# A decoder trunk on one core: the second MLP product's queues in the order of emission, its raw weight halves kept by use, and two mixer weights read into rows of another tile

## The chip, the cores and the metric

The kernel is one program for one core of one Trainium2 chip. The metric is the device time of one execution in microseconds (us); lower is better. Before the change it is 2401.24 us, the median of three runs (2396.24 to 2403.47).

The engines are called by the names of the profile: PE multiplies matrices (PEld is its weight load), DVE and ACT do elementwise work, POOL does a few small things, and SP issues nearly all transfers (DMAs) between the core's memory and DRAM. Each engine runs its own instructions in a fixed order and waits at the first whose inputs or buffers aren't ready. Matmuls write into PSUM, which has eight banks of 128x512 numbers; DVE and ACT have to read a bank out ("evict" it) before PE may start another sum in it.

## The reference

Two layers on a residual stream of 1024 positions by 1024 channels. What matters here is the MLP, which both layers have, and the weights of the second layer's attention:

```python
def _sqrelu_mlp(x, w_up, w_down):                       # 1024 -> 4096 -> 1024
    return jnp.square(jax.nn.relu(x @ w_up)) @ w_down
...
for i in range(DEPTH):
    m = gmlp(...) if i % 2 == 0 else diff_attention(...)   # attention: qkv = a @ w_qkv
    h = h + _rmsnorm(m, g_mix_post[i])
    f = _sqrelu_mlp(_rmsnorm(h, g_ffn_pre[i]), f_w_up[i], f_w_down[i])
    h = h + _rmsnorm(f, g_ffn_post[i])
    gate = jax.nn.sigmoid(_rmsnorm(h, g_ple_pre[i]) @ ple_w_gate[i] + ple_b_gate[i])
    e = gate * (p[i] @ ple_w_proj[i])
    h = h + _rmsnorm(e, g_ple_post[i])
```

## The kernel before

**Arithmetic.** Everything is fp32. Each operand is cut into a high part (ACT copies it to the matmul's type) and a low part (DVE subtracts the high part from the whole), and each product is three matmuls, high by high, high by low and low by high (lines 352 to 354 in `mm3`, line 364 in `proj_steps`). Cutting one operand is thus one ACT and one DVE instruction: `cut` in `ffn` (line 523 on ACT, line 524 on DVE), `split` for the other stages (lines 113 to 120).

**The MLP** is `ffn`, called once per layer. Both of its products are done with seven half-size products in place of eight, so sums and differences of blocks have to be formed. The first product (`product`, `block`) forms blocks of the hidden activations, squares them and stores seven kinds of them to DRAM (`hid`). The banks of the first product are read out by `plus` (line 601), on DVE.

**The second product** is the loop at line 810. It has 56 steps in four groups: groups 0, 1 and 2 have 16 steps each (steps 0 to 47), group 3 has 8. In each step PE does 24 matmuls of 128x128 by 128x512: four output rows `p`, two banks each, three matmuls per bank. All eight banks are in use: `PM[p]` and `other[p]` hold one group's sums through its 16 steps. After a group's last step `evict(g, p)` reads the two banks of each row out into halves of the rows of `MA` (lines 785 to 796): one ACT and one DVE instruction per row in group 0, two DVE ones in group 1 (lines 789 and 790), three in group 2. The next group's first matmul into a bank has to wait for that.

**Feeding the steps.** For step `n`, `load_down(n)` issues the transfers and `split_down(n)` does the arithmetic. The call `after(t)`, at the end of step `t`, first calls `split_down` for the step that is `lead_s` ahead (two in group 0, three in groups 1 and 2) and then `load_down` for the one that is `lead_l` ahead (seven through step 50). The places that the cut operands go to are seven rooms, used in turn, so the loads of step `n` into its room have to wait for PE to be done with step `n - 7`. In `load_down`, group by group:

- groups 0 and 1: a whole row block of the weight (512 KB, line 727) and one half of another (256 KB, line 728) into a set of raw buffers, and a slice of `hid` (512 KB, line 729) into the room;
- group 2: two halves (256 KB each, line 724) and a half `t4` that group 1 has stored to DRAM (256 KB, line 725) into raw buffers, and the slice of `hid`.

The raw buffers of a group are a ring of sets in `sets` (five in groups 0 and 1, in the order of the steps; four in group 2). A set is one whole 128x1024 buffer and one half of a row of `MA`.

`split_down` forms two differences on DVE (lines 746 and 747 in group 1, 753 and 754 in group 2), issues a store of one of them to `t4` from SP in the middle of its own work (lines 748 and 755), and cuts three pieces: the `hid` slice (128x1024) and two weight halves (128x512).

**What sets the order.** The code emits instructions in the order of its loops, but only PE keeps that order (the whole trunk stands in `tc.manual_schedule(engines={PE})`, line 1319). The order on SP, ACT, DVE and POOL is made when the program is built, by a planner that takes instructions as it expects them to be ready, the earlier emitted first among those that are. On the chip this order is then fixed. Inside a block of `manual_schedule` the instructions of the engines that it names keep their order of emission among themselves; instructions emitted outside the block may still be placed between them.

**Around it.** In group 3 and after it, `half` and `whole` scale and sum the rows, add them to the residual and prepare the next stage, whose transposes (line 296) PE does when `settle` asks for them or when `tick` has counted far enough.

**Mixer weights.** The other stages read their weights through `ws` (`WStream`): `load` reads a 512 KB block (line 88) into the next of a ring of raw buffers and splits it into one of six slots, and `take` hands four of them out. At the start of `mixer1` (line 1158) the first two blocks of `w_qkv` are already in their slots; the other two of the first four are loaded when `qkv_qk` first calls `take`, through the ring `[raw, hin[0], hin[1]]` set at line 1165. `hin` also holds the residual rows of the stage before (`residual`, lines 336 to 342). The rows of `MA` hold that stage's outputs until PE has transposed them, row by row.

Of the kernel before, what the change touches and what calls it, by code (L numbers as in the profile page):

```python
# [21 lines left out]
NT = T // P  # L22
# [3 lines left out]
NQ = DFF // FB  # L26
# [17 lines left out]
def f32(ap):  # L44
    return ap.bitcast(F32)
# [86 lines left out]
def _trunk(ctx, tc, nc, a, out):  # L132
# [14 lines left out]
    MA = sp.tile([P, NT, D], F32, name="ma")  # L147
    WT = [sp.tile([P, 2, D], F32, name=f"w{i}") for i in range(4)]
    hin = [sp.tile([P, D], F32, name=f"hin{i}") for i in range(2)]
# [116 lines left out]
    def settle(key=None):  # L266

        while put_off and (key is None or any(k == key for k, _, _ in put_off)):
            put_off.popleft()[2]()
# [245 lines left out]
    def ffn(i, hsrc, hdst, next_weights):  # L515
# [6 lines left out]
        def cut(h, l, v):  # L522
            act(h, v, AF.Copy)  # L523
            vec(out=l, in0=v, in1=f32(h), op=sub)  # L524
# [124 lines left out]
        def stream():  # L649
            for q in range(NQ):  # L650
                if q < 3:
                    settle((4, 6, 7)[q])
                yield from load_up(q)

        LEAD = 6
        loads = stream()
        early = [(q, n) for qs in ((0, 1), (2,), (3,), (4,)) for n in (1, 2) for q in qs]
        stage = [x.rearrange("p (r k f) -> p r k f", r=2, f=P) for x in (raw, bbc, raw, bbc, bbc)]
# [37 lines left out]
        def cols(x, k):  # L696
            return x[:, k * 512:k * 512 + 512]
# [1 line left out]
        sets = [  # L699
            Ring([(MA[:, 1], cols(MA[:, 2], 0)), (MA[:, 3], cols(MA[:, 2], 1)), (raw, cols(MA[:, 4], 0)),  # L700
                  (MA[:, 5], cols(MA[:, 4], 1)), (MA[:, 6], cols(bbc, 0))]),
            Ring([(x, cols(MA[:, t], 1)) for t, x in zip((0, 7, 2, 3, 4), hin + [xn[0], raw, bbc])]),
            Ring([(x, cols(MA[:, t], 1)) for t, x in zip((6, 5, 4, 7), [hin[1], raw, bbc, hin[0]])]),
        ]


        sumR = Ring([cols(xn[1], k) for k in range(2)])
        steps = [(g, c) for g in range(4) for c in range(NQ if g < 3 else NQ // 2)]
        loaded, cuts, ssq = {}, {}, {}

        def load_down(n):
            g, c = steps[n]
            room = last[c] if g == 3 else rooms[n % 7]
            hi, lo = [f32r(x.rearrange("p k t -> p (k t)")) for x in room]
            wh, hh, wl, hl = hi[:, 0:1024], hi[:, 1024:], lo[:, 0:1024], lo[:, 1024:]
            x = sets[g].next() if g < 3 else None
            if g == 3:
                for k in range(2):
                    nc.sync.dma_start(f32(cols(hl, k)), hid[2 * c + k][:, 3072:])
                nc.sync.dma_start(f32(wl), t4[c])  # L720
            else:
                if g == 2:
                    for k in range(2):
                        nc.sync.dma_start(cols(x[0], k), down[c, k, 1])
                    nc.sync.dma_start(x[1], cols(t4[c // 2], c % 2))
                else:
                    nc.sync.dma_start(x[0], down_rows[c, 0])
                    nc.sync.dma_start(x[1], down[c, 1, 1 - g])
                nc.sync.dma_start(f32(hl), hid[c][:, g * 1024:g * 1024 + 1024])
            loaded[n] = wh, wl, hh, hl, x  # L730

        def split_down(n):
            g, c = steps[n]
            wh, wl, hh, hl, x = loaded.pop(n)
            if g < 3:
                a1, a2 = cols(x[0], 0), cols(x[0], 1)
            if g == 0:

                t = sumR.next()
                vec(out=t, in0=a2, in1=a1, op=sub)  # L740
                vec(out=a2, in0=x[1], in1=t, op=sub)
                w = x[0],
            elif g == 1:

                t = sumR.next()
                vec(out=t, in0=a2, in1=a1, op=sub)
                vec(out=a1, in0=x[1], in1=a1, op=sub)
                nc.sync.dma_start(cols(t4[c // 2], c % 2), a1)
                w = x[1], t
            elif g == 2:  # L750

                t = sumR.next()
                vec(out=t, in0=a2, in1=a1, op=sub)
                vec(out=x[1], in0=x[1], in1=t, op=sub)
                nc.sync.dma_start(cols(t4[c // 2], c % 2), x[1])
                w = t, a2
            else:
                w = f32(wl),
            cut(hh, hl, f32(hl))
            k = D // len(w)  # L760
            for j, v in enumerate(w):
                cut(wh[:, j * k:j * k + k], wl[:, j * k:j * k + k], v)
            cuts[n] = wh, wl, hh, hl

        def after(t):

            for n in range(len(steps)):
                if n - t == lead_s[n]:
                    split_down(n)
            for n in range(len(steps)):  # L770
                if n - t == lead_l[n]:
                    load_down(n)

        for k, n in enumerate(rest_of):
            next(loads, None)
# [28 lines left out]
        def whole(tt, us):  # L804
# [2 lines left out]
            rstd_of(s[:, 0:1], D, RMS_EPS)  # L807
            residual(tt, MA[:, tt, :], s[:, 0:1], hsrc, hdst, us)

        for m, (g, c) in enumerate(steps):  # L810
            wh, wl, hh, hl = cuts.pop(m)
            n_c = NQ if g < 3 else NQ // 2

# [344 lines left out]
    def mixer1(gi, hsrc, hdst):  # L1158
# [3 lines left out]
        nc.gpsimd.dma_start(sgc, a["subln"])  # L1162
        nc.vector.tensor_scalar(out=sgc, in0=sgc, scalar1=1.0 - LAMBDA_INIT, scalar2=None, op0=ALU.mult)
        pbR.i = 2 * (pmR.i % 3)
        ws.raws = Ring([raw] + hin)
        for cb in range(2):
            qkv_qk(cb, qD, HD ** -0.5, cosT, sinT)
# [267 lines left out]
```

## Time and profile before

| what | value |
| --- | --- |
| median of three runs | 2401.24 us |
| the profiled execution: time, span in the profile | 2402.34 us, 2400.6 us |
| DVE busy over the span | 1609.3 us (67%) |
| ACT busy over the span | 1165.4 us (49%) |
| second product of layer 0, steps 0 to 55 | about 606 to 938 us |
| second product of layer 1, steps 0 to 55 | about 1951 to 2280 us |
| end of the gate stage, start of `mixer1` | about 1055 us |

All times inside the profile are us from the start of the span. In a timeline row the first number is the start, the second the duration, then come engine, line, operation, tiles (written <- read) and shape; the bracket at the end is the time that the engine was idle just before, and what ended it. In a row of waits stand the engine, tile and line that waited, what ended the wait, the us in total, the number of times and the longest. A row of windows gives, for a stretch, the busy time and the number of instructions of each engine, the granted PE clock (1.00 is full), the share of the 16 DMA engines and GB/s. Matmuls overlap, so a busy duration of 0.39 us goes with a distance of about 0.23 us between starts.

### The profile page before, as it was taken

Reading aid. Unit: us, or ns where it says so; the run is one execution under the profiler, and the core shown is the slowest. Engines: PE = TensorE matmul, PEld = TensorE weight load, DVE = VectorE, ACT = ScalarE, POOL = GpSimd, SP = SyncE. Lnnn points to the kernel's source line nnn. Section 1 sums busy time; section 2 is a strip of 40 time slices with the busy share of each in tenths; the row PEclk is TensorE's granted clock in tenths of the full one; section 3 lists DMA queues with packets and bytes.
Section 4 is the critical chain, followed back from the end, with each engine's and each line's share of the span. In section 5 each row is a group of like instructions: output and inputs, shape, how many; then the busy total and the mean of one; then the engine's idle time right before and its main releaser. Section 6 shows DMA issues by size and latency. Waiting matters only on the chain. (4 is left out here: it accounts for less than half of the span.)

```text
span 2400.6 us, 30544 instructions
## 1 busy us (share of the span) xinstructions
PE 2327.9 (97%) x10748; PEld 1924.2 (80%) x10748; DVE 1609.3 (67%) x2492; ACT 1165.4 (49%) x2003; POOL 228.0 (9%) x303
## 2 busy tenths in 40 slices
PE   9999999999999899999999989999999999989998
PEld 7888888888788687878887878777888888868787
DVE  4733697777866765563335888868877797675654
ACT  6232575555433355462224666657555554334551
POOL 1100100000000022010001342321000000000310
PEclk9999999999999999999999999999999999999999
DMA  9111545446977765244445765554544588777423
GB/s 330 57 35 54 165 142 202 145 156 223 355 249 236 250 233 183 74 169 142 147 154 179 218 181 143 158 184 137 189 159 164 173 335 279 243 256 245 176 106 123
DMA packets 200425, 441.03 MB, mean 184 GB/s; under 512 B 21040, under 2 KB 55856, under 8 KB 200144
## 3 DMA queue, kind: packets, MB, share of 16 engines
q1 hardware_dynamic: 199840, 437.89, 54.4%
q8 instruction: 85, 1.39, 0.2%
q0 software_dynamic: 432, 1.19, 0.2%
q14 instruction: 68, 0.56, 0.1%
HBM read 310.02 MB, written 133.17 MB: 185 GB/s over the span
## 5 line engine op out<-in xcount | busy, mean ns | idle before, releaser
L364 PE MATMUL pm_a<-w,xh 128*128 128x512 f32 x704 | 223.9, 396 | 1.3 <-ACT w L119 0.9
L364 PEld LDWEIGHTS pm_a<-w,xh 128*128 128x128 f32 x704 | 131.6, 189 | 29.8 <-ACT w L119 2.6
L523 ACT ACTIVATE xh<-xl 128x1024 fp32r<-128x1024 f32 x72 | 75.4, 1055 | 148.9 <-DMA xl<-hid 137.5
L364 PE MATMUL pb<-w,xh 128*128 128x512 f32 x416 | 134.9, 400 | 5.5 <-DVE gbc L972 2.9
L524 DVE TENSOR_TENSOR xl<-xl,xh 128x1024 fp32r<-128x1024 f32 x72 | 87.4, 1221 | 78.6 <-ACT xh L523 75.6
L364 PE MATMUL pm_a<-w,xl 128*128 128x512 f32 x352 | 138.7, 394 | 0.0
L523 ACT ACTIVATE w<-ma 128x512 fp32r<-128x512 f32 x130 | 82.2, 634 | 115.6 <-PE pm_a L353 39.5
L524 DVE TENSOR_TENSOR s<-s 128x1024 fp32r<-128x1024 f32 x56 | 68.0, 1222 | 58.9 <-ACT s L523 58.9
L523 ACT ACTIVATE s<-s 128x1024 fp32r<-128x1024 f32 x56 | 58.5, 1054 | 97.6 <-DMA s<-hid 80.6
L847 POOL DMA_DIRECT2D bbc<-in_ple_b_gate_dram x2 | 1.3, 628 | 1077.1 <-DVE s L524 1077.1
L353 PE MATMUL pm_a<-xl,w 128*128 128x512 f32 x260 | 101.4, 390 | 0.2 <-DVE xl L283 0.2
L352 PE MATMUL pm_a<-xh,w 128*128 128x512 f32 x260 | 101.6, 391 | 0.0
L354 PE MATMUL pm_a<-xh,w 128*128 128x512 f32 x260 | 101.2, 389 | 0.0
L364 PEld LDWEIGHTS pb<-w,xh 128*128 128x128 f32 x416 | 77.1, 190 | 20.1 <-DVE xn L394 3.4
L524 DVE TENSOR_TENSOR w<-ma,w 128x512 fp32r<-128x512 f32 x130 | 88.6, 683 | 0.7 <-ACT w L523 0.7
L243 POOL TENSOR_SCALAR small<-small 128x1 f32<-128x1 f32 x104 | 34.7, 333 | 553.9 <-DVE small L397 322.0
L340 DVE SCALAR_TENSOR_TENSOR hin<-ma,small,hin 128x1024 f32<-128x1024 f32 (+1 forms) x49 | 61.6, 1260 | 37.0 <-DMA hin<-h 24.5
L364 PE MATMUL pb<-w,xl 128*128 128x512 f32 x208 | 82.9, 399 | 0.0
L352 PE MATMUL pb<-xh,w 128*128 128x512 f32 x204 | 79.7, 391 | 0.0
L354 PE MATMUL pb<-xh,w 128*128 128x512 f32 x204 | 79.4, 389 | 0.0
L353 PE MATMUL pb<-xl,w 128*128 128x512 f32 x204 | 79.4, 389 | 0.0
L364 PEld LDWEIGHTS pm_a<-w,xl 128*128 128x128 f32 x352 | 66.4, 189 | 12.9
(476 smaller groups left out, 7048.2 us busy)
## 6 DMA issues: line engine op xcount, KB each, us to landing
xl<-hid SPq DMA_DIRECT2D x56, 512.0 KB, 5.1
ma<-in_f_w_up_dram SPq DMA_DIRECT2D x48, 512.0 KB, 3.7
h<-hin SPq DMA_DIRECT2D x40, 512.0 KB, 3.1
hid<-ma SPq DMA_DIRECT2D x80, 256.0 KB, 2.4
s<-hid SPq DMA_DIRECT2D x40, 512.0 KB, 5.2
hin<-h SPq DMA_DIRECT2D x40, 512.0 KB, 3.5
hid<-xn SPq DMA_DIRECT2D x64, 256.0 KB, 2.6
hid<-hin SPq DMA_DIRECT2D x64, 256.0 KB, 2.7
```

The source lines that it names most:

```text
L243: nc.gpsimd.tensor_scalar(out=ss, in0=ss, scalar1=1.0 / n, scalar2=eps, op0=ALU.mult, op1=ALU.add)
L340: nc.vector.scalar_tensor_tensor(out=h[:, cs], in0=t_ap[:, cs], scalar=rs, in1=h[:, cs], op0=ALU.mult, op1=ALU.add)
L352: nc.tensor.matmul(ps, lhsT=lh, rhs=rh, start=start, stop=False)
L353: nc.tensor.matmul(ps, lhsT=lh, rhs=rl, start=False, stop=False)
L354: nc.tensor.matmul(ps, lhsT=ll, rhs=rh, start=False, stop=stop)
L364: nc.tensor.matmul(ps, lhsT=xs(l, kc, tt * P), rhs=r[:, cs], start=kc == 0 and k == 0, stop=kc == KC - 1 and k == 2)
L523: act(h, v, AF.Copy)
L524: vec(out=l, in0=v, in1=f32(h), op=sub)
L847: nc.gpsimd.dma_start(bbc, a["ple_b_gate"][i:i + 1, :].broadcast_to([P, D]))
```

## The change

It has three parts.

1. **Order.** From step 0 to step 44 of the second product (`FREE = 3 * NQ - 3 = 45`) SP, ACT and DVE keep the order of emission, as PE did before. From step 9 on `after` emits the loads first, then the stores to `t4`, then the splits; the stores are collected in a list by `split_down` and emitted by the next `after`.
2. **Raw buffers.** In groups 1 and 2 each 256 KB half has a ring of its own: eight places for the half that is also stored to `t4`, five for each of the two others in group 1; seven and five in group 2. The whole row block of group 1 becomes two loads of one half each. In group 2 the half read back from `t4` goes into the room (`wl`), after the `hid` slice, and the difference is written over the raw half.
3. **Mixer weights.** At the start of `mixer1`, ahead of the projections, two blocks of `w_qkv` are loaded through `MA[:, 2]` and `MA[:, 3]`.

```diff
+        FREE = 3 * NQ - 3
...
         sets = [
             Ring([(MA[:, 1], cols(MA[:, 2], 0)), ... (MA[:, 6], cols(bbc, 0))]),
-            Ring([(x, cols(MA[:, t], 1)) for t, x in zip((0, 7, 2, 3, 4), hin + [xn[0], raw, bbc])]),
-            Ring([(x, cols(MA[:, t], 1)) for t, x in zip((6, 5, 4, 7), [hin[1], raw, bbc, hin[0]])]),
         ]
+        h0, h1, rw, bb, x0 = [[cols(x, k) for k in range(2)] for x in (*hin, raw, bbc, xn[0])]
+        ma = [cols(MA[:, t], 1) for t in range(NT)]
+        thirds = {
+            1: ([h0[0], h1[0], x0[0], rw[0], bb[0], ma[3], ma[2], ma[1]],
+                [x0[1], h0[1], h1[1], rw[1], ma[5]],
+                [ma[0], ma[7], bb[1], ma[4], ma[6]]),
+            2: ([ma[7], rw[0], h0[0], h1[0], bb[1], ma[4], bb[0]],
+                [h0[1], h1[1], rw[1], ma[5], ma[6]] * 3 + [h0[1]]),
+        }
...
-            x = sets[g].next() if g < 3 else None
+            x = sets[0].next() if g == 0 else [r[c % len(r)] for r in thirds.get(g, ())]
...
                 if g == 2:
                     for k in range(2):
-                        nc.sync.dma_start(cols(x[0], k), down[c, k, 1])
-                    nc.sync.dma_start(x[1], cols(t4[c // 2], c % 2))
+                        nc.sync.dma_start(x[k], down[c, k, 1])
+                elif g == 1:
+                    for k in range(2):
+                        nc.sync.dma_start(x[k], down[c, 0, k])
+                    nc.sync.dma_start(x[2], down[c, 1, 0])
                 else:
                     nc.sync.dma_start(x[0], down_rows[c, 0])
-                    nc.sync.dma_start(x[1], down[c, 1, 1 - g])
+                    nc.sync.dma_start(x[1], down[c, 1, 1])
                 nc.sync.dma_start(f32(hl), hid[c][:, g * 1024:g * 1024 + 1024])
+                if g == 2:
+                    nc.sync.dma_start(f32(cols(wl, 0)), cols(t4[c // 2], c % 2))
...
                 vec(out=t, in0=a2, in1=a1, op=sub)
-                vec(out=a1, in0=x[1], in1=a1, op=sub)
-                nc.sync.dma_start(cols(t4[c // 2], c % 2), a1)
-                w = x[1], t
+                vec(out=a1, in0=x[2], in1=a1, op=sub)
+                w = x[2], t
...
-                vec(out=x[1], in0=x[1], in1=t, op=sub)
-                nc.sync.dma_start(cols(t4[c // 2], c % 2), x[1])
+                vec(out=a1, in0=f32(cols(wl, 0)), in1=t, op=sub)
                 w = t, a2
...
+            if g in thirds:
+                stores.append((cols(t4[c // 2], c % 2), a1))
...
         def after(t):
+            def begin():
+                for n in range(len(steps)):
+                    if n - t == lead_l[n]:
+                        load_down(n)
+            def store():
+                while stores:
+                    nc.sync.dma_start(*stores.pop(0))
+            if t + 7 >= NQ:
+                begin()
+                store()
             for n in range(len(steps)):
                 if n - t == lead_s[n]:
                     split_down(n)
-            for n in range(len(steps)):
-                if n - t == lead_l[n]:
-                    load_down(n)
+            if t + 7 < NQ:
+                begin()
+            if t >= FREE:
+                store()
...
+        E = mybir.EngineType
+        strict = tc.manual_schedule(engines={E.PE, E.SP, E.Activation, E.DVE})
+        strict.__enter__()
         for m, (g, c) in enumerate(steps):
+            if m == FREE:
+                strict.__exit__(None, None, None)
...
         pbR.i = 2 * (pmR.i % 3)
+        ws.raws = Ring([MA[:, 2, :], MA[:, 3, :]])
+        settle(3)
+        for _ in range(2):
+            ws.load()
         ws.raws = Ring([raw] + hin)
```

More of the change, by code (lines that the diff above doesn't have):

```diff
@@ L701, in ffn @@
                   (MA[:, 5], cols(MA[:, 4], 1)), (MA[:, 6], cols(bbc, 0))]),
-            Ring([(x, cols(MA[:, t], 1)) for t, x in zip((0, 7, 2, 3, 4), hin + [xn[0], raw, bbc])]),
-            Ring([(x, cols(MA[:, t], 1)) for t, x in zip((6, 5, 4, 7), [hin[1], raw, bbc, hin[0]])]),
-        ]
+        ]
+        h0, h1, rw, bb, x0 = [[cols(x, k) for k in range(2)] for x in (*hin, raw, bbc, xn[0])]
[7 more added lines that the diff above has]
+        }
         sumR = Ring([cols(xn[1], k) for k in range(2)])
         steps = [(g, c) for g in range(4) for c in range(NQ if g < 3 else NQ // 2)]
-        loaded, cuts, ssq = {}, {}, {}
+        loaded, cuts, ssq, stores = {}, {}, {}, []
         def load_down(n):
@@ L735, in split_down @@
             if g < 3:
-                a1, a2 = cols(x[0], 0), cols(x[0], 1)
+                a1, a2 = x[:2] if g else (cols(x[0], 0), cols(x[0], 1))
             if g == 0:
```

## The prediction, made before the changed kernel had run

> **What bounds the kernel now.** I read the page first, then the list of waits for PE alone, then windows around the places that the list named.
>
> ```profile
> span 2400.6 us, 30544 instructions
> PE 2327.9 (97%) x10748; PEld 1924.2 (80%) x10748; DVE 1609.3 (67%) x2492; ACT 1165.4 (49%) x2003; POOL 228.0 (9%) x303
> ```
>
> PE is the bound: no other engine passes 67%. What can be won without taking matmuls away are PE's stops, and the list of PE's waits names them:
>
> ```profile
> PE pt L296 <- DVE xl L283: 8.9, 3, 4.1
> PE pm_c L352 <- DVE ma L789: 8.3, 2, 8.1
> PE pm_a L352 <- DVE ma L789: 7.6, 1, 7.6
> PE pm_a L352 <- ACT s L119: 4.5, 1, 4.5
> PE pm_a L352 <- DVE hin L601: 2.3, 1, 2.3
> ```
>
> Line 789 is the eviction after group 1, one long stop per layer; line 119 is the split of a mixer weight; line 601 is the last eviction of the first product; line 296 are the transposes at the end of the MLP. Windows that hold a stop, and a stretch without one beside them, price the stops:
>
> ```profile
> 605.50:780.00 174.50, 171.73 (x748) 141.29 (x749) 124.07 (x158) 69.96 (x92) 0.00 (x0) 0.99 0.81 276
> 780.00:805.00 25.00, 17.24 (x61) 12.91 (x60) 20.17 (x31) 10.96 (x20) 0.00 (x0) 0.80 0.68 232
> 805.00:885.00 80.00, 80.00 (x354) 66.25 (x353) 51.93 (x67) 34.28 (x47) 3.41 (x3) 1.00 0.77 251
> 1950.90:2122.00 171.10, 169.64 (x749) 140.11 (x748) 124.00 (x158) 70.64 (x93) 0.00 (x0) 1.00 0.80 281
> 2122.00:2150.00 28.00, 19.39 (x73) 14.44 (x72) 23.27 (x35) 11.99 (x22) 0.00 (x0) 0.82 0.79 256
> ```
>
> The undisturbed pace is 80.00 / 354 = 0.226 us per matmul, so a step of 24 takes about 5.45 us. At this pace the 61 matmuls of the second row need 13.8 us of its 25.0, so the stop at the group boundary costs **11.2 us** in layer 0; the 73 of the last row need 16.5 of 28.0, **11.5 us** in layer 1. Both hold more than the wait itself, since the granted clock is 0.80 and 0.82 there: PE restarts slowly. The first and fourth rows give 174.5 - 748 x 0.226 = 5.4 us and 171.1 - 749 x 0.226 = 1.8 us lost in steps 0 to 31, nearly all at the entry (line 601).
>
> Why was the bank of line 789 read out so late? Layer 1, DVE's timeline, with ACT's row between:
>
> ```profile
> 2127.89 1.23 DVE L524 TENSOR_TENSOR xl<-xl,xh 128x1024 fp32r<-128x1024 f32 x1 [3.01 <-ACT xh L523]
> 2129.03 0.68 DVE L524 TENSOR_TENSOR s<-xn,s 128x512 fp32r<-128x512 f32 x1
> 2129.64 0.68 DVE L524 TENSOR_TENSOR s<-hin,s 128x512 fp32r<-128x512 f32 x1
> 2130.24 0.68 DVE L753 TENSOR_TENSOR xn<-bbc 128x512 f32<-128x512 f32 x1
> 2130.96 0.69 DVE L754 TENSOR_TENSOR ma<-ma,xn 128x512 f32<-128x512 f32 x1
> ...
> 2131.44 1.06 ACT L523 ACTIVATE s<-s 128x1024 fp32r<-128x1024 f32 x1 [2.54 <-DMA s<-hid]
> ...
> 2132.53 1.23 DVE L524 TENSOR_TENSOR s<-s 128x1024 fp32r<-128x1024 f32 x1 [0.88 <-ACT s L523]
> 2134.27 0.68 DVE L789 TENSOR_TENSOR ma<-pm_c,ma 128x512 f32<-128x512 f32 x1
> ```
>
> DVE was not short of time: it idled 3.01 us for a cut while PE stood. In its fixed order the eviction comes after cuts for steps that PE reaches four steps later (the rooms' names repeat in a cycle of seven, which makes the slice of 2131.44 that of step 36, with PE at step 32), and those cuts waited for their `hid` slices. The slices were late because of SP:
>
> ```profile
> 2125.63 0.38 SPq L755 DMA_DIRECT2D t<-ma  x1
> 2126.11 0.38 SPq L729 DMA_DIRECT2D s<-hid  x1
> 2130.19 0.32 SPq L725 DMA_DIRECT2D ma<-t  x1
> ...
> SPq L725 <- DMA t<-ma: 70.0, 24, 5.1
> ```
>
> Line 725 stands until the store of line 755 has landed, since it fills the same buffer: 24 waits, 70.0 us. The slice of step 36 could have gone when PE left step 29, two steps (10.9 us) before 2126.8, but was issued at 2126.11.
>
> **The change part by part.**
>
> *Order.* DVE comes to line 789 with only the splits up to step 33 ahead of it. These don't hang on steps 30 or 31, so DVE stands ready and reads each bank when PE leaves it. The 11.2 and 11.5 us go. What is added is a wait: DVE stands at line 789 until PE is through, and behind it are queued the splits from step 34 on, for which PE waits next. Their cover: eviction ends two DVE instructions after PE's last matmul of step 31 (2130.24 to 2130.96 and on, 0.6 to 0.7 us each), 1.4 us. From the rows above a split is 1.14 + 0.61 + 0.60 + 0.72 + 0.60 = 3.7 us of DVE. So step 34 is ready 5.1 us after step 31, and PE wants it after two steps, 10.9 us: 5.8 us to spare, and every further step gains 5.45 - 3.7 = 1.75 us. The four `half` instructions in steps 34 to 37 take 0.6 us each out of that. The wait costs nothing; were the cover gone, it would cost what a split is late, up to its 3.7 us per boundary. After group 0 there is one DVE eviction per row in place of two, so more is spare. ACT goes through the same order with less work.
>
> SP now stands at each `hid` slice until PE has left the step seven back, and the stores and the next step's halves are queued behind. A slice issued then lands after 5.2 us, then 1.06 us of ACT and 3.7 of DVE: some 10 us of a lead of six steps (32.7 us).
>
> *Raw buffers.* SP's wait at line 725 goes: the read-back goes into the room and a store has two steps or more to land before its half is filled again. The rings of five make a load wait for the split five steps back; that lies two steps ahead of PE, and after the eviction of group 1 it is split 34, ready 5.1 us after step 31 where SP asks for it at 5.45. What is late next on SP is PE itself. Group 1 has 16 more transfers per layer, each some 0.5 us of SP (2125.63 to 2126.11), on a queue that stands most of each step, and the bytes are the same. Whether two short transfers cost more than a long one:
>
> ```profile
> hin<-in_f_w_down_dram SPq DMA_DIRECT2D x32, 256.0 KB, 3.9
> hin<-in_f_w_down_dram SPq DMA_DIRECT2D x14, 512.0 KB, 4.6
> s<-hid SPq DMA_DIRECT2D x40, 512.0 KB, 5.2
> ```
>
> A half lands in 3.9 us, a whole block in 4.6, both issued several steps before use and in flight together. From nothing to 0.7 us per step at worst (were landings in series), 16 x 0.7 = 11 us a layer; four steps between load and split hide it, and I take nothing. The Trainium skill, "DMA: Bandwidth & Descriptors", section "Anatomy of one DMA", speaks against such splitting: about 2.0 us fixed per transfer and the bytes at 436 GB/s, by which two halves take an estimated 5.2 us where a block takes 3.2, and 16 steps of two layers would lose an estimated 64 us if transfers went one by one. The rows disagree: a transfer twice as large took 0.7 us longer, not 1.2, and the fixed part overlaps with others in flight.
>
> *Mixer weights.* The stop at line 119:
>
> ```profile
> 1042.57 0.60 PE L296 MATMUL pt<-identr,ma 128*128 128x128 f32 x4
> 1050.99 0.39 PE L364 MATMUL pm_a<-s,xl 128*128 128x512 f32 x1
> 1060.11 0.40 PE L354 MATMUL pm_a<-xh,s 128*128 128x512 f32 x1
> 1064.99 0.80 PE L352 MATMUL pm_a<-xh,s 128*128 128x512 f32 x1 [4.48 <-ACT s L119]
> 1068.50 0.40 PE L354 MATMUL pm_a<-xh,w 128*128 128x512 f32 x1
> 1078.55 0.60 PE L296 MATMUL pt<-identr,ma 128*128 128x128 f32 x4
> ...
> 1059.87 0.33 SPq L88 DMA_DIRECT2D hin<-in_w_qkv_dram  x1
> ...
> 1064.21 1.33 ACT L119 ACTIVATE s<-hin,gcol 128x512 fp32r<-128x512 f32 x2 [1.28 <-DMA hin<-in_w_qkv_dram]
> 1067.53 1.15 ACT L330 ACTIVATE ma<-hin,small 128x1024 f32<-128x1024 f32 x1 [0.94 <-POOL small L244]
> ```
>
> The fourth block was read at 1059.87, when the residual row had left `hin`, and split at 1064.21; its slot was free from 1050.99 + 0.39. Through `MA[:, 3]`, whose transposes, row 3's, end at 1043.2 (the first row), the split can stand right after 1051.4; ACT and DVE need 1.3 and 1.4 us, so it is there by about 1055, ahead of 1060.3. From 1060.11 to 1068.50 lie nine starts in 8.39 us where 9 x 0.226 = 2.0 would do: **6.3 us** go. `settle(3)` brings nothing forward, as those rows were transposed long before. Next late would be row 7's transposes, which come at 1078.55 now and some 6 us sooner then, against data ready at 1067.53 + 1.15 = 1068.7: no stop.
>
> Sum, against the profiled execution of 2402.3 us: 11.2 + 11.5 + 6.3 = 29.0, so 2373.3. The median of the runs shown is 1.1 us lower: **2372 us**. I leave the entry (5.4 and 1.8 us) and the transposes of line 296 as they are: the evictions of line 601 were emitted outside the ordered block, so ordered splits may still be placed before them, and line 296 falls into steps after 44.
>
> **The rivals.**
>
> *The entry goes too* (0.15). If the planner no longer puts splits of steps 2 to 6 before line 601, another 5.4 + 1.8 = 7.2 us go: 2365. For it: DVE's work there changes its order. Against it: those splits are ready early, as before.
>
> *A smaller wait in its place* (0.17). DVE or SP standing for PE at a boundary makes the next split late after all. PE's entry wait shows what a short stop costs:
>
> ```profile
> 609.54 0.50 PE L352 MATMUL pm_a<-xh 128*128 128x512 f32 x1 [2.35 <-DVE hin L601]
> 611.43 0.63 PE L353 MATMUL pm_a<-xl,xh 128*128 128x512 f32 x1
> 611.86 0.63 PE L354 MATMUL pm_a<-xh,xl 128*128 128x512 f32 x1
> ```
>
> 2.35 us of idling, and 1.9 us later starts are 0.43 apart, so some 4 us in all; at the two boundaries of two layers up to 16, I take 11: 2383. The Trainium skill, "TensorE: Matmul & The Clock Gate", Part 1, puts the slow clock behind about 3.4 us of idling; by that rule a stop of 2.35 us would cost itself alone (an estimate of 9 us for four). Here the rows show slow starts after 2.35 us, so I go by the rows.
>
> *The mixer's part stays out* (0.08), if SP's queue has the load behind a residual store that waits: 2372 + 6 = 2378.
>
> *The change doesn't do what it says* (0.08): if evictions are late for another reason than their place in DVE's order, the boundaries stay and only the mixer's part or less is won: 2396 to 2401. Against it: DVE idled ahead of line 789.
>
> *Transfers become the bound, slower* (0.08). At PE's full pace a step of groups 1 and 2 moves six times 256 KB, 1.57 MB in 5.45 us: 288 GB/s, and the rows show 276 and 281 at shares of 0.81 and 0.80 with late slices. If more, shorter rows in a fixed order held the engines below that, each of the 29 steps 16 to 44 would be longer; four steps of lead (22 us) hide the first part. It decides from (22 + 11.3 + 3.2 + 3.6) / 29 = 1.4 us per step, 6.85 us or 230 GB/s; at 220 it is 7.15 us, 49 - 22 = 27 us a layer, that is 54 more than forecast: about 2426. Against it: over 171 us the queue moved 281. The section of "DMA: Bandwidth & Descriptors" in the Trainium skill named above is the rule that speaks for this rival.
>
> **How the numbers follow.** The forecast has 0.44, the rivals 0.15, 0.17, 0.08, 0.08, 0.08. A measurement of this kernel tells about 0.3% (7.2 us) from no change. Faster than 2394 are the forecast and the first three rivals: 0.84; same 0.08, of the fourth; slower 0.08. The range runs from 2360, the entry rival with 5 us for the end of the MLP coming out better in the planner's new order, to 2392, the smaller wait at its upper price with the mixer's part half won; it leaves out the last two cases and a little of the others, 0.2.
>
> **What would show it.** Right: in PE's waits both rows of line 789 and the one of line 119 fall below 1 us; windows around the group boundaries have a clock of 1.00; SP's waits of line 725 for `t` are gone, and SP waits for PE at line 729's place. Wrong: a new row in PE's waits for line 524 within groups 1 or 2 (splits late), a DMA share near 0.9 there with steps longer than 5.5 us, or longer waits at line 601 or 296 that give the time back.

## The result, and the profile after

| | time | ratio to the kernel before, 95% interval |
| --- | --- | --- |
| before | 2401.76 us median (2396.24 to 2404.12, 6 runs) | |
| after | 2374.35 us median (2369.49 to 2382.26, 6 runs) | 0.9884 (0.987 to 0.9898) |

The forecast was 2372 us. The profiled execution took 2373.64 us, where the sum of the prediction had 2373.3. First the page of the changed kernel, busy time of each engine:

```profile
span 2371.9 us, 30550 instructions
PE 2320.3 (98%) x10748; PEld 1921.0 (81%) x10748; DVE 1605.2 (68%) x2492; ACT 1167.1 (49%) x2003; POOL 240.5 (10%) x303
```

The span is 28.7 us shorter, PE's work the same. PE's waits after the change (engine, line, what ended the wait; us in total, times, longest):

```profile
PE pt L296 <- DVE xl L283: 6.7, 5, 1.6
...
PE pt L296 <- ACT ma L330: 4.0, 2, 2.0
...
PE pm_c L352 <- DVE ma L822: 2.1, 2, 1.7
...
PE pm_a L352 <- DVE ma L822: 1.0, 2, 0.8
...
PE pm_a L352 <- DVE hin L601: 0.4, 1, 0.4
```

Line 789 of the kernel before is line 817 here (790 is 818, 792 to 794 are 820 to 822), and it has no row any more; the row of a mixer weight on line 119 is gone, and those of the entry, line 601, fell from 4.5 us (2.3, 1.5 and 0.7) to 0.4, where the forecast had left them as they were. New is a row for the transposes of line 296 that wait for ACT's line 330. Windows over the same stretches of the two second products, from the entry to past the boundary of groups 1 and 2 (PE, PEld, DVE, ACT, POOL; clock, DMA share, GB/s):

```profile
605.50:780.00 174.50, 174.10 (x769) 143.88 (x768) 122.05 (x157) 67.57 (x87) 0.00 (x0) 1.00 0.84 275
780.00:805.00 25.00, 25.00 (x112) 20.72 (x111) 24.79 (x36) 15.08 (x26) 0.00 (x0) 1.00 0.88 281
...
2101.00:2129.00 28.00, 28.00 (x125) 23.20 (x124) 27.79 (x40) 14.64 (x26) 0.00 (x0) 1.00 0.92 288
```

PE has no gap at the boundaries and the clock is 1.00 there. In layer 0 the boundary now falls at about 775 to 779 us, inside the first row; between 780 and 805 us PE did 112 matmuls where it had done 61. DVE's timeline at layer 1's boundary shows it standing ready, idle until PE leaves the first bank:

```profile
2100.50 0.69 DVE L817 TENSOR_TENSOR ma<-pm_c,ma 128x512 f32<-128x512 f32 x1 [12.52 <-PE pm_c L354]
```

The wait of 12.52 us is the one that the change adds, and nobody waits behind it. SP's waits: the 70.0 us for `t` are gone, and at the `hid` slices (line 742, before 729) SP now waits for PE, which was 38.1 us in 29 waits before:

```profile
SPq L742 <- PE pt L354: 232.2, 80, 4.1
```

Where did the 28.7 us come from? I cut both traces at the first matmuls of each stage. The end of an MLP is counted from the start of step 47's last matmul to the first matmul of the gate stage (line 364), and entry and boundary by the time that starts of matmuls stand more than 0.3 us apart, less the pace of 0.227 us.

| stretch | before | after | difference |
| --- | --- | --- | --- |
| layer 0, MLP | 641.3 | 629.5 | -11.8 |
| - of it the entry | 5.1 | 0.7 | -4.4 |
| - the boundary of groups 1 and 2 | 11.4 | 0 | -11.4 |
| - the end | 55.0 | 60.0 | +5.0 |
| gate stage and mixer | 701.4 | 694.4 | -7.0 |
| layer 1, MLP | 641.1 | 631.3 | -9.8 |
| - of it the entry | 1.7 | 0 | -1.7 |
| - the boundary | 12.0 | 0 | -12.0 |
| - the end | 54.8 | 59.9 | +5.1 |

So the two boundaries and the mixer came out as forecast, and beside them **two things that the forecast left out cancel in part**: the entry won 6.1 us and the end of the MLPs lost 10.1; the rest, 3.0 us won, are small pieces. Windows over the end of layer 0's MLP, before and after, say more of what was lost there:

```profile
882.99:938.00 55.01, 49.65 (x227) 40.44 (x226) 33.91 (x45) 30.41 (x50) 20.68 (x22) 0.97 0.48 172
866.11:926.13 60.02, 53.69 (x227) 42.28 (x226) 38.07 (x53) 33.63 (x55) 27.29 (x22) 0.91 0.49 176
```

For the same number of recorded matmuls (227) PE was busy 4.0 us longer, at a granted clock of 0.91 in place of 0.97, and stood only 1.0 us longer. In layer 1 it was busy 3.0 us longer (clock 0.94 in place of 0.97) and stood 2.1 us longer. So 7.0 of the 10.1 us are matmuls that ran slower, and 3.1 are stops. The experiments ask what each part is worth, and why the entry and the end moved.

### The profile page after: what moved, and what is told of

Read it like the earlier page. It is cut to its first block, busy times and chain, and to the rows that moved or that the text cites. A ratio compares the mean times of both kernels' runs of the same rounds, so it can differ in the third digit from the quotient of the medians.

```text
span 2371.9 us, 30550 instructions
## 1 busy us (share of the span) xinstructions
PE 2320.3 (98%) x10748; PEld 1921.0 (81%) x10748; DVE 1605.2 (68%) x2492; ACT 1167.1 (49%) x2003; POOL 240.5 (10%) x303
## 3 DMA queue, kind: packets, MB, share of 16 engines
q1 hardware_dynamic: 204448, 437.89, 55.6%
## 4 chain that ended last, share of the span: by engine, by line
PE 86%; DVE 6%; DMA 4%; ACT 2%; issue 2%; POOL 1%; SPq 0%; DVEq 0%; POOLq 0%; ACTq 0%
PE pm_a L364 12%; PE pb L364 7%; PE pm_a L352 7%; PE pm_a L354 7%; PE pm_a L353 7%; PE pb L354 6%; PE pb L352 6%; PE pb L353 6%; PE pm_c L352 5%; PE pm_c L354 5%; PE pm_c L353 5%; PE pm_c L364 3%; PE pt L353 2%; PE pt L352 2%; PE pt L354 2%
## 5 line engine op out<-in xcount | busy, mean ns | idle before, releaser
L244 POOL TENSOR_TENSOR small<-small,mhalf 128x1 f32<-128x1 f32 x104 | 77.1, 742 | 8.4
```

Of the source, the lines that this page charges most:

```text
L244: nc.gpsimd.tensor_tensor(out=ss, in0=ss, in1=mhalf[:, :k], op=ALU.pow)
```

## The experiments

All ratios are to the kernel before, measured on the same chip with the kernel. Its median was 2404.11 us for the first four kernels, 2403.26 for the one with VectorE alone in order and the three with less work at the end of group 2, and 2405.39 for the one with the entry alone and the three with another end of the order. Kernels of different sets are compared by their ratios. VectorE, ScalarE and GpSimd are the names of DVE, ACT and POOL outside the profile.

### The mixer's part alone

The kernel before with only the third part:

```diff
+        ws.raws = Ring([MA[:, 2, :], MA[:, 3, :]])
+        settle(3)
+        for _ in range(2):
+            ws.load()
         ws.raws = Ring([raw] + hin)
```

> The kernel before with the change's third part alone (two blocks of w_qkv through MA rows 2 and 3). If the parts add up, as the sum in the prediction says: 6.3 us off, about 2395.5, with the row of PE waiting for line 119 at pm_a below 1 us and the waits of line 789 as before (7.6 and 8.3 us). Rival, that the mixer's stop is covered by a later one: no change, 2401 to 2403, and another row of PE's waits grown by some 4 us.

Measured: 2397.03 us, 0.9972 (0.9962 to 0.9981), 6.7 us. In PE's waits the boundary stays and line 119's row for a mixer weight is gone:

```profile
PE pm_a L352 <- DVE ma L789: 9.9, 2, 9.7
...
PE pm_c L352 <- DVE ma L789: 6.5, 2, 6.3
```

The term of 6.3 us holds and stands by itself.

### The order with the old raw buffers

The kernel before with the ordered block alone, `after` as it was:

```diff
+        strict = tc.manual_schedule(engines={E.PE, E.SP, E.Activation, E.DVE})
+        strict.__enter__()
         for m, (g, c) in enumerate(steps):
+            if m == 3 * NQ - 3:
+                strict.__exit__(None, None, None)
```

> The kernel before with the ordered block alone (SP, ACT, DVE to step 44), with its old raw buffers, the store in the middle of the split and the loads after the splits. Theory A, that the place of the evictions in DVE's order cost the 11 us at each boundary: both stops of line 789 gone, about 2402 - 22.7 - 7 (entry) + 9 (end) = 2381. Theory B, that the late hid slices did it, because SP stands for the stores: the ordered SP now stands for each split and each store before it loads, so slices stay late, splits come late and PE has stops at line 524 in groups 1 and 2: 2395 or more.

Measured: 2391.62 us, 0.9952 (0.9939 to 0.9965). The boundary of groups 1 and 2 is clean, and a stop of that size stands **at the next one**, behind group 2:

```profile
PE pm_c L352 <- DVE ma L794: 12.1, 1, 12.1
PE pm_a L352 <- DVE ma L794: 11.4, 1, 11.4
```

The time lies between the two theories' figures. The boundary went as theory A has it; of theory B's sign, stops of PE at line 524, there are none. SP's waits of the read-back were still 82.0 us in 24 waits, and the slices of steps 32 to 36 were issued 6.8 to 7.6 us apart where PE's step is 5.45. What stood ahead of the late eviction behind group 2, in layer 0, were two splits of gate weights (line 120) and a cut of group 3, whose slices SP issued at 869.73 us and later, behind loads of gate weights (line 88). Late transfers thus made a stop at the next place, but they are not the same transfers: these are emitted after the ordered block has ended.

### The new buffers without the order, and the order without DVE

Two kernels from the changed one, which differ from it in the engines that the block names:

```diff
-        strict = tc.manual_schedule(engines={E.PE, E.SP, E.Activation, E.DVE})
+        strict = tc.manual_schedule(engines={E.PE})
```

> The changed kernel without the ordered block: new rings, late stores and the mixer's part, with the order on SP, ACT and DVE left to the planner. Theory A: evictions still stand behind splits four steps ahead, so the stops after group 1 stay at several us each: 2390 to 2397, of which the mixer's part makes 6.3. Theory B: slices are on time, so the splits ahead of line 817 don't wait: stops below 1 us, about 2372 to 2380.

Measured: 2390.23 us, 0.9953 (0.9938 to 0.9968). Theory A holds. The eviction is late again, behind twelve of group 2's differences (seven first and five second ones):

```profile
PE pm_a L352 <- DVE ma L817: 5.4, 1, 5.4
PE pm_c L352 <- DVE ma L817: 3.5, 1, 3.5
```

The other names SP and ScalarE and leaves VectorE to the planner (`engines={E.PE, E.SP, E.Activation}`).

> The changed kernel with only SP and ACT in order, DVE left to the planner. Theory A: the stops after group 1 come back at least in part (2 to 11 us each), 2378 to 2395. Theory B: SP is on time, so they stay away, 2372 to 2376.

Measured: 2378.32 us, 0.9898 (0.9876 to 0.992), whose interval overlaps that of the changed kernel. The time is above theory B's range and at the edge of theory A's; the waits decide between them. VectorE's eviction stood behind eleven differences of group 2 (six first and five second ones; seven pairs in the kernel before, two in the changed one), and yet:

```profile
PE pm_c L352 <- DVE ma L817: 0.8, 1, 0.8
...
PE pm_a L352 <- DVE ma L817: 0.5, 1, 0.5
...
SPq L742 <- PE pt L354: 238.6, 78, 4.4
```

(The first rows are PE's, the last is SP's.) This corrects my reading of the trace of before. A late place in DVE's order cost under 1 us as long as the slices that the work ahead of it needs were there; to cost 11 us it took slices that SP issued late as well. No run put SP in order without ACT, so ACT's share in this isn't separated.

### VectorE alone in order

The changed kernel with `engines={E.PE, E.DVE}`.

> The changed kernel with only DVE in order, SP and ACT left to the planner. After the earlier runs the theory is that a stop at a boundary needs two things, evictions behind splits of later steps and late hid slices. With DVE in order the first is missing at the end of group 1, so no stop of several us at line 817; if slices are late, they show at line 822 (end of group 2, outside the ordered block), as with the old buffers: 2376 to 2392. Rival, that late slices alone suffice: splits come late, PE stops at line 524 in group 2.

Measured: 2385.88 us, 0.9931 (0.9913 to 0.9948). As with the old buffers, the boundary is clean and the stop stands behind group 2:

```profile
PE pm_c L352 <- DVE ma L822: 12.6, 1, 12.6
PE pm_a L352 <- DVE ma L822: 10.6, 1, 10.6
```

VectorE's timeline ahead of that eviction in layer 0 has the same work as with the old buffers, a gate weight's split and a cut of group 3, both late:

```profile
871.94 1.41 DVE L120 SCALAR_TENSOR_TENSOR w<-raw,gcol,w 128x512 fp32r<-128x512 f32 x2 [4.48 <-ACT w L119]
874.72 2.36 DVE L524 TENSOR_TENSOR xl<-xl,xh 128x1024 fp32r<-128x1024 f32 x2 [1.37 <-ACT xh L523]
```

SP issued the slices of that cut at 867.91 and 868.82 us, behind two loads of gate weights (line 88, 861.76 and 867.48). PE had come to the end of step 47 at 867.45 us, much as in the changed kernel (866.11), so it had lost nothing in groups 1 and 2.

Order and buffers each alone leave a stop of 3.5 to 12 us in each layer; with both, no stop for an eviction of the second product is longer than 1.7 us. The totals say the same less clearly: order with old buffers won 11.5 us (0.0048 x 2404); new buffers without order won 11.3, of which 6.7 are the mixer's; the whole change won 27.9 (0.0116 x 2402), 21.2 without the mixer, against 11.5 + 4.6. The 5.1 us between are less than the intervals of the three ratios add up to.

### The entry alone

The kernel before, ordered in steps 0 to 7 only (as above, with `if m == 8:`).

> The kernel before, with SP, ScalarE and VectorE in the order of emission during steps 0 to 7 alone. Theory (VectorE's place of the early splits against line 601's evictions makes the entry's loss): the excess over PE's pace in the first steps falls from 5.1 and 1.7 us to about 1.1 and 0.3, the stops of line 789 (8.1 and 7.6 us) and of line 119 stay; ratio about 0.9978, some 5 us faster than before. Rival (the entry went because the loads of the new buffers run earlier): 5.1 and 1.7 us stay, ratio 1.000.

Measured: 2399.53 us, 0.9978 (0.9967 to 0.999). The excess at the entry fell to 0.5 us in layer 0 and below 0.3 in layer 1, the boundaries stayed. So the entry's gain is the order's, not the buffers'. And it is VectorE's order: with VectorE alone in order the entry lost about 1 and 0.3 us, with SP and ScalarE in order and VectorE left free 3.7 and 1.0. DVE's timeline of the kernel before shows what it stood behind, and that of the changed kernel what is left:

```profile
604.73 0.68 DVE L601 TENSOR_TENSOR gbc<-pm_a,hin 128x512 f32<-128x512 f32 x1
605.33 1.22 DVE L524 TENSOR_TENSOR s<-ma,s 128x1024 fp32r<-128x1024 f32 x1
606.46 0.69 DVE L741 TENSOR_TENSOR ma<-ma,xn 128x512 f32<-128x512 f32 x1
607.06 1.22 DVE L524 TENSOR_TENSOR xl<-xl,xh 128x1024 fp32r<-128x1024 f32 x1
608.20 0.69 DVE L740 TENSOR_TENSOR xn<-ma 128x512 f32<-128x512 f32 x1
608.80 0.68 DVE L601 TENSOR_TENSOR hin<-pm_a,hin 128x512 f32<-128x512 f32 x1
```

```profile
603.37 0.68 DVE L601 TENSOR_TENSOR gbc<-pm_a,hin 128x512 f32<-128x512 f32 x1
603.97 0.68 DVE L756 TENSOR_TENSOR ma<-ma,xn 128x512 f32<-128x512 f32 x1
604.57 1.21 DVE L524 TENSOR_TENSOR xl<-xl,xh 128x1024 fp32r<-128x1024 f32 x1
605.71 0.68 DVE L601 TENSOR_TENSOR hin<-pm_a,hin 128x512 f32<-128x512 f32 x1
```

Four pieces of splits stood between the last two evictions of the first product, two are left, and the last one comes 3.1 us earlier.

### Less work at the end of group 2

Three tries at the end's 10 us, on the theories that VectorE had too much to do there or had the wrong things ahead of the evictions: the second halves of rows 4 to 7 later, the loads of the gate stage's weights two steps later, and both. The edits of both:

```diff
-                for p in range(4):
-                    half(p + 4, 1)
+            if g == 3 and c < 4:
+                half(c + 4, 1)
...
-                if c < 4:
+                if 2 <= c < 6:
                     ws.load()
-                elif c < 6:
+                if 4 <= c < 6:
```

> The changed kernel with the four scalings of the second halves of rows 4 to 7 (ACT and DVE, line 830) moved from the end of step 47 to steps 48 to 51. In the changed kernel the first rstd of the rows stands on POOL for 5.55 us where it takes 0.55 alone, all the while DVE is without a gap; the stops at line 296 (6.7 and 4.0 us in all) follow from that. Theory P, POOL's small operations are held up by DVE's unbroken work: four instructions of 0.6 us less just then, the stops shrink, 1 to 5 us off, 2369 to 2373. Rival Q, the end is set by what the planner puts ahead of the evictions (splits of gate weights, line 120): no change, 2373 to 2376.

> The changed kernel with the four loads and splits of gate weights emitted two steps later (after steps 50 to 53 in place of 48 to 51). Theory Q: fewer splits of line 120 ahead of and among the evictions of group 2, stops at line 822 (1.0 and 2.1 us) shrink and the rows' chain starts earlier: 2 to 6 us off, 2368 to 2372. Theory P: some of the same gain, as DVE has 5.6 us less to do then. If neither, the planner still hoists them: 2374.

> Both moves of the two kernels beside it. Theories P and Q alike: 3 to 9 us off the changed kernel, 2365 to 2371, the most if both hold; with the stops at line 296 below 5 us in all where they are 10.7 now.

Measured: 2376.23 us, 0.9888 (0.987 to 0.9905); 2374.01 us, 0.9879 (0.9864 to 0.9894); 2374.86 us, 0.9884 (0.9867 to 0.99). None differs from the changed kernel, and none of the gains that theories P and Q had forecast came. With the loads later, the waits of line 822 shrank to 0.7 and 0.6 us, while those of line 296 rose from 10.7 (6.7 + 4.0) to 13.2 (9.2 + 4.0): the loss moved by one wait and stayed. The ends took 60.2 and 60.6, 59.1 and 59.5, 61.3 and 60.2 us.

### Where the order ends

The changed kernel with the block ended at another step (`FREE = 34`, 40 or 47 in place of 45). The stores to `t4` follow `FREE` too: from that step on they are emitted right after the splits and not by the next `after`, so these kernels move both. In the last expectation, 47 is two steps later than in the changed kernel; what it calls GpSimd's small sums are the steps of lines 243 and 244, a scaling and a power. The 59.2 and 59.7 us that the first expectation gives for the ends of the changed kernel are 60.0 and 59.9 as counted here.

> The changed kernel with the ordered block ended at step 34, two steps after the boundary of groups 1 and 2. Theory (the order near the end of group 2 is what makes the end 59.2 and 59.7 us long instead of 55.0 and 54.9): the boundary stays without a stop, the end goes back to about 55 us, some 9 us less than the changed kernel, 2365. Rival 1 (the end is longer because PE arrives there without having stopped, with the same work still to do on VectorE and GpSimd): 59 to 60 us, the time within 3 us of 2374. Rival 2 (the planner's order puts the third group's evictions behind other work again): a stop at line 822 of 3 to 12 us per layer, 2380 to 2395.

> The changed kernel with the ordered block ended at step 40. Theory (order makes the end): about 55 us and 2365; rival 1 (PE's early arrival makes it): 59 to 60 us and 2374; rival 2 (evictions late): stops at line 822, 2380 or more.

> The changed kernel with the ordered block ended at step 47, three steps before the changed kernel's bound would be passed by two. VectorE then stands for PE at the end of group 2, with gaps in which GpSimd's small sums take about 0.55 us and not 5.55. Theory (GpSimd's slow sum makes the stop at the first transposes): that stop of 2.0 us goes, the end shortens by about 2 us a layer, 2370. Rival (the rows' work is late behind ordered splits): the end grows by 3 to 10 us a layer, 2380 to 2394.

| block ends at step | time | ratio, 95% interval | ends of the MLPs |
| --- | --- | --- | --- |
| 34 | 2365.98 us | 0.9842 (0.9824 to 0.986) | 56.7, 55.9 us |
| 40 | 2378.95 us | 0.9895 (0.9877 to 0.9914) | 60.1, 62.8 us |
| 45 (the change) | 2374.35 us | 0.9884 (0.987 to 0.9898) | 60.0, 59.9 us |
| 47 | 2368.15 us | 0.9852 (0.9833 to 0.9871) | 56.0, 55.6 us |

**At 34 the kernel beats the one before and the changed one**; its interval lies below that of the changed kernel, while that of 47 just touches it. Its boundary stays clean (0 and 0.7 us lost), since the order holds there up to two steps past it. The rival that PE's early arrival makes the end longer has fallen: in layer 0 PE ends step 47 at 867.8 and 866.5 us with 34 and 47, at 866.1 in the changed kernel and at 883.0 in the one before, and of these four only the changed kernel's end is long. But my theory, the order near group 2's end as such, isn't right either, since 40 is as bad as 45 and 47 is good. The good ones have the first eviction of group 2 earlier, as the timeline of DVE and PE at the end of step 47 shows. First the changed kernel:

```profile
864.12 1.22 DVE L524 TENSOR_TENSOR xl<-xl,xh 128x1024 fp32r<-128x1024 f32 x1
...
865.25 0.74 DVE L120 SCALAR_TENSOR_TENSOR w<-raw,gcol,w 128x512 fp32r<-128x512 f32 x1
865.91 0.68 DVE L820 TENSOR_TENSOR ma<-pm_a,ma 128x512 f32<-128x512 f32 x1
866.11 0.39 PE L354 MATMUL pt<-xh,xl 128*128 128x512 f32 x1
```

then the kernel before:

```profile
879.42 0.68 DVE L792 TENSOR_TENSOR ma<-pm_a,ma 128x512 f32<-128x512 f32 x1
...
882.99 0.39 PE L354 MATMUL pt<-xh,xl 128*128 128x512 f32 x1
```

and the block ended at 34:

```profile
864.98 0.69 DVE L820 TENSOR_TENSOR ma<-pm_a,ma 128x512 f32<-128x512 f32 x1
...
867.77 0.39 PE L354 MATMUL pt<-xh,xl 128*128 128x512 f32 x1
```

The last row of each is the last matmul of step 47. Row 0's banks are done 18 matmuls, 4.1 us, before it. So group 2's first eviction came 866.11 - 4.1 = 862.0, 3.9 us late, in the changed kernel; 0.5 us late in the one before; 1.3 with the block ended at 34. In the changed kernel it stands behind cuts of the next group's steps and a gate weight's split (line 120), which wait for transfers. Over all fourteen kernels profiled, two MLPs each:

| first eviction of group 2 late by | MLPs | their ends |
| --- | --- | --- |
| 0.4 to 2.0 us | 10 | 54.8 to 56.7 us |
| 2.1 to 3.9 us | 14 | 55.3 to 62.8 us (11 of them over 59) |
| 13.6 to 15.6 us | 4 | 63.0 to 68.0 us |

So a late first eviction mostly goes with a long end, but it doesn't decide it. Both MLPs of the kernel with new buffers and no order had it 3.0 and 3.7 us late, and their ends took only 57.2 and 55.3 us, at a clock of 0.97. With the block ended at 47 the later evictions came late instead: PE stood 3.5 and 3.6 us at line 822, and yet the ends took 56.0 and 55.6, at 1.00 and 0.97. In the changed kernel three short stops at the transposes (2.0, 1.5 and 1.6 us) stand where the kernel before has one of 4.1, and its clock was lower. No run changed the eviction or the stops alone, so what makes the end longer stays open; how much of it is clock and how much stops is what the windows in the result show.

The last expectation also asked whether GpSimd's slow step (line 244, the power in the rows' scaling) makes the stop at the first transposes. The timeline of the changed kernel has this chain:

```profile
882.05 5.55 POOL L244 TENSOR_TENSOR small<-small,mhalf 128x1 f32<-128x1 f32 x1
...
887.95 0.55 POOL L244 TENSOR_TENSOR small<-small,mhalf 128x1 f32<-128x1 f32 x1
...
889.44 1.15 ACT L330 ACTIVATE ma<-hin,small 128x1024 f32<-128x1024 f32 x1 [5.77 <-POOL small L244]
...
890.64 0.72 PE L296 MATMUL pt<-identr,ma 128*128 128x128 f32 x3 [2.01 <-ACT ma L330]
```

and with the block ended at 34:

```profile
881.35 5.55 POOL L244 TENSOR_TENSOR small<-small,mhalf 128x1 f32<-128x1 f32 x1
...
889.03 0.66 PE L296 MATMUL pt<-identr,ma 128*128 128x128 f32 x4 [1.16 <-ACT ma L330]
```

With 47 there is no stop for line 330, and the longest of GpSimd's small steps is 4.30 us. But with 34 the step of 5.55 us is still there and the end is 56.7. The step takes part in the chain, it doesn't decide the end.

## Why the prediction came out as it did

The total was right to 2 us. Three of its terms are the larger part of why, and luck is the rest, since two others weren't in it.

- **The boundaries** (11.2 and 11.5 us forecast): 11.4 and 12.0. Size and place are right. I wrote that the eviction's place in DVE's order, behind cuts for later steps, made the stop, and named SP's late slices as why those cuts waited. The stop needs both, and taking away either clears this boundary: with SP and ACT in order and DVE left to the planner the place alone cost under 1 us, and with only DVE in order, or with order and old buffers, there was no stop here at all. What the forecast didn't see is that the order alone isn't enough: those last two kernels stood 10.6 to 12.6 us behind group 2, where evictions outside the ordered block came behind late gate weights and a late slice.
- **The mixer** (6.3): 6.7 alone by the ratio's middle (4.6 to 9.1 by its interval), 6.2 up to the first scores in the changed kernel's trace.
- **The added wait at line 817** was costed at nothing, with 5.8 us to spare. It holds: 12.52 us of waiting on DVE in layer 1, and no wait of PE for line 524 in either group.
- **Sixteen more transfers** were costed at nothing. A 256 KB load of the weight now lands after a median of 4.6 to 5.5 us, by buffer (5.5 into `hin`), where before it took 3.9 to 4.7 (3.9 into `hin`). The steps between load and use hide that; had the landing not been covered, it would have shown as waits for line 524. The share of the DMA engines rose to 0.92 at the boundary while the steps kept their 5.45 us, so of the sign that I had named for the transfers as the bound, a share near 0.9 with longer steps, only the first half came. By the rule of the Trainium skill ("DMA: Bandwidth & Descriptors", section "Anatomy of one DMA") quoted there, two halves would have cost an estimated 64 us more if transfers went one by one. That section gives its figures for transfers that GpSimd issues, and these are SP's; nothing of that size is in the trace.
- **The entry** failed: "I leave the entry (5.4 and 1.8 us) ... as they are: the evictions of line 601 were emitted outside the ordered block, so ordered splits may still be placed before them". They may, and half as many are. That rival had 0.15; the run with the entry alone shows its mechanism and won 5 us. Of the 5.1 us in layer 0, 1.6 are slow starts: the kernel with the mixer's part alone has the same stops without them, and lost 3.5.
- **The end** failed: the same sentence left line 296 as it was, because it "falls into steps after 44". It lost 10.1 us. The mistake was to treat what lies behind the ordered block as untouched, and to look at its stops alone: PE's waits at line 296 shown above grew from 8.9 to 10.7 us (6.7 + 4.0), while 7.0 of the 10.1 us were matmuls at a lower clock. Moving the end of the order changed the end of the MLP by up to 7 us in a layer; through which step of the chain stays open. The range had taken "the end of the MLP coming out better" as its lower bound and nothing for its coming out worse.

A total that fits is no proof of its terms: -6.1 and +10.1 hid each other, with 3.0 us of small gains beside them. That they came so close to zero is luck.

## What to carry to other kernels

Fix the order of a queue together with what feeds it: with transfers that came late, a fixed order on the engine that evicts cleared one stop here and left one behind the next group, where its block had ended. Where a hand-written order ends is a parameter of its own, with 13 us between the best and the worst step tried here, so try a few. Look at PE's granted clock beside its waits, since most of what the end lost stood in no row of waits. And compare a forecast with the trace stage by stage, since a matching total can hold two errors.

## What the hardware showed that was not expected

**GpSimd and VectorE hold each other up.** The same 128x1 power on GpSimd took 0.55 us and 5.55 us in the same execution (the two POOL rows of line 244 above, though spans on POOL are rough). During the long one VectorE worked without a gap. The next instruction after that stretch, in the changed kernel, has VectorE's idling in its bracket:

```profile
894.28 1.29 DVE L340 SCALAR_TENSOR_TENSOR hin<-ma,small,hin 128x1024 f32<-128x1024 f32 x1 [7.09 <-DMA hin<-h]
```

VectorE's stretch ended at 887.19 us (894.28 less 7.09) and the power at 887.60, 0.41 us later; with the block ended at 34 these are 886.49 and 886.90, 0.41 us again. It goes the other way too, in the kernel before:

```profile
882.22 5.22 POOL L114 TENSOR_TENSOR s<-s 128x1024 fp32r<-128x1024 f32 x2 [33.16 <-ACT s L113]
885.09 2.36 DVE L806 TENSOR_TENSOR small<-small 128x1 f32<-128x1 f32 x1
...
889.77 0.14 DVE L806 TENSOR_TENSOR small<-small 128x1 f32<-128x1 f32 x1
```

VectorE's 128x1 sum took 2.36 us and ended at 887.45, as GpSimd's split did at 887.44; alone it took 0.14. The Trainium skill, "SBUF — State Buffer", section "SBUF: two separate sides", has a lock for this: an operation of GpSimd and one of VectorE with two inputs from SBUF can't run side by side, and the second one waits for the first to end. VectorE's 2.36 us agree. GpSimd's 5.55 us don't: the longest single instruction of VectorE in that time took 1.28 us, so GpSimd waited out a whole run of them.

**How long PE stood doesn't tell whether it slows.** PE's timeline behind the stop of 2.01 us at the first transposes of the changed kernel, then behind a stop of 3.48 us in layer 0 with the block ended at 47:

```profile
891.23 0.77 PE L352 MATMUL pm_a<-xh 128*128 128x512 f32 x1
891.80 0.63 PE L353 MATMUL pm_a<-xl,xh 128*128 128x512 f32 x1
892.22 0.63 PE L354 MATMUL pm_a<-xh,xl 128*128 128x512 f32 x1
```

```profile
875.78 0.51 PE L352 MATMUL pm_a<-s 128*128 128x512 f32 x1 [3.48 <-DVE ma L822]
876.12 0.39 PE L353 MATMUL pm_a<-s 128*128 128x512 f32 x1
```

Starts are 0.57 and 0.42 us apart behind the shorter stop, and the granted clock was 0.50 from 890.9 to 894.3 us. Behind the longer one they are 0.34 and then 0.23 apart, and the clock was 1.00 from 875 to 880; in layer 1 of that kernel a stop of 3.60 us did have slow starts. The same stop needn't do the same twice either: the entry's stop of 2.35 us in layer 0, from which the prediction took the price of a short stop, had slow starts in the kernel before and none in the kernel with the mixer's part alone (2.35 us, at 608.85). The Trainium skill, "TensorE: Matmul & The Clock Gate", Part 1, has the clock fall after about 3.4 us of idling; these rows have slow starts after less, and none after 3.48. What decides it isn't shown here, so the price of a stop is best read from the granted clock behind it.
